# Layer 0's mixers: list scheduling of noted instructions, second parts of weights by adding DMAs, decayed states as products

## The chip, the cores and the metric

The kernel is one program on one core of a Trainium2 chip. A core has five engines with a queue each, worked through in order: TensorE (PE), VectorE (DVE), ScalarE (ACT), GpSimd (POOL) and SyncE (SP, which here only issues DMAs). They meet through semaphores. The metric is the device time of one execution in microseconds, the median of several runs. All times by stage come from one profiled execution.

## The reference, cut to what matters

```python
# layer 0 (even)
z = rmsnorm(h, mix_norm) @ mix_w_in                       # (512, 1024) @ (1024, 3328)
y_a = rwkv7_bidir(z[..., :RWKV_COLS], ...)                # 8 heads x 64, both directions
y_b = hyena_bidir(z[..., RWKV_COLS:], ...)                # 512 channels, long filters by FFT
h = h + concatenate([y_a, y_b], -1) @ mix_w_out
# the scan in rwkv7_bidir, one step
sa = einsum('dbhvk,dbhk->dbhv', S, kk_t)
S = S * w_t[..., None, :] - sa[..., :, None] * (kk_t * a_t)[..., None, :] + v_t[..., :, None] * k_t[..., None, :]
y_t = einsum('dbhvk,dbhk->dbhv', S, r_t)
# the rest, after the mixers of layer 0
h = h + conv_ffn(h, ...); h = h + per_layer_embedding(h, ...)
# layer 1: neighbourhood attention, conv_ffn, per_layer_embedding in the same manner
```

512 tokens, width 1024, everything in float32. What the change touches is `y_a` and `y_b`, the input projection before them, and some work of later parts that runs beside them.

## The kernel before, in words

**Products in two parts.** A large product is made of float32r matmuls of 128x128 by 128x512. Weights and activations are split in a rounded first part (`xh`, `whi`) and a second part, the rest (`xl`, `wlo`); `mm3` sums three matmuls: first by first, first by second, second by first. In the mixers a weight comes in pieces of 128x512 (256 KB), called items. `stream` loads an item to a slab, ACT casts it to the first part (line 570), and GpSimd subtracts that from the loaded item to get the second (`parts`, a subtraction of line 356). The tables of the transform have both parts in HBM: two loads, a cast on ACT (597) and one on GpSimd (598).

**The mixers.** `mixer0` holds 59 slabs of 128x520 in SBUF and eight PSUM banks. The work is: `norm0` (squares on ACT, their sum over 1024 rows on DVE, four one-column matmuls, then rstd); `low_rank` and `columns` (the projection, 26 column groups of 24 large matmuls, two items each); for each of four head pairs m `rwkv_in`, two `rwkv_prep` (one per direction), `inverse_ab` (a block inverse: 15 steps of row substitution on DVE, then small matmuls; it goes through HBM twice), `scan` and `rwkv_out`; for Hyena `hyena_in`, `filters`, `filter_parts`, `forward`, `signals`, `spectrum`, `inverse`, `hyena_out`; and beside them `embedding` (products of the embeddings for both layers, stored for later) and `out_early` (part of the output projection, from the first three head pairs).

**One chunk of a scan.** A scan goes through 512 tokens in eight chunks of 64, both directions and both heads of a pair at once. In a chunk PE multiplies the state tile `uv` by `m1`, DVE copies the result out of PSUM to `r0` (1267), PE multiplies by the inverse `zt`, ACT and DVE write the negated result to the two halves of `uv` (359, 1282), PE multiplies by the keys `x`, and DVE adds the decayed old state `sp` in two operations, one for each half (`uv<-b,sp`). `sp` itself, the state times the chunk's decay `pcs`, is two multiplications on DVE earlier in the chunk. Up to two scans run at once.

**What sets the order.** All functions are generators. `drive` pulls them: `main` is the list of projections, transforms and embeddings in a written order; `chains` are the other parts with a priority each. `Pace` keeps an estimate of when each engine is free and each tile is done. At each point `drive` takes the first chain whose tiles are ready, or, when PE's recent work is thin, the next step of `main`. `in_order` then fixes that order on each engine.

**The end.** After the mixers `outproj0` loads h back (1539), loads the late rows of the output weight (`wraw<-in_mix_w_out_b`, 378), splits them and multiplies. From there on the program runs feed-forward, embedding, attention and again feed-forward.

Lines: 350 is every `mm`, 353 every `stt`, 356 every `tt`, 359 every `act`, 364 the cast of `split`.

Of the kernel before, what the change touches and what calls it, by code (L numbers as in the profile page):

```python
# [19 lines left out]
P = 128  # L20
# [184 lines left out]
class Pace:  # L205


    HOP, OWN = 0.2, 0.13

    def __init__(self, nc):  # L210
        self.nc = nc
        self.free, self.done, self.used = {}, {}, {}
        self.dma = 0.0
        self.columns = {}
        self.recent = deque()
        self.pending = {}
        self.n = len(nc.cur_bb.bb.instructions)

    @staticmethod
    def name(t):  # L220
        return t if isinstance(t, str) else getattr(t, "tensor", t).name

    @staticmethod
    def area(x):

        size = math.prod(x.tensor.shape[1:])
        p, f = divmod(x.offset, size)
        p1, f1 = p, f
        for i, (step, n) in enumerate(x.ap):
            if i == 0 and step == size:  # L230
                p1 += n - 1
            elif step < 0:
                f += step * (n - 1)
            else:
                f1 += step * (n - 1)
        return x.tensor.name, (p, p1, f, f1)

    def now(self, engine=None):
        self.update()
        return self.free.get((engine or self.nc.tensor).engine, 0.0)  # L240

    def ready(self, tiles):

        self.update()
        return max((math.inf if self.pending.get(n) else max(self.done.get(n, {}).values(), default=0.0)
                    for n in map(self.name, tiles)), default=0.0)

    def after(self, marks, area, e, own):

        t = 0.0  # L250
        name, (p, p1, f, f1) = area
        for (k, (q, q1, g, g1)), v in marks.get(name, {}).items():
            if p <= q1 and q <= p1 and f <= g1 and g <= f1:
                if k != e:
                    t = max(t, v + self.HOP)
                elif own:
                    t = max(t, v + self.OWN)
        return t
# [4 lines left out]
    def cold(self, t):  # L263
        return self.columns.get(int(t / self.TICK) - 1, 0) < self.COLUMNS

    def density(self, t):

        while self.recent and self.recent[0][0] < t - self.TICK:
            self.recent.popleft()
        return sum(c for _, c in self.recent)  # L270

    def cost(self, ins, op, n):
        nc, e = self.nc, ins.engine
        if e == nc.tensor.engine:
            passes = 1 if ins.ins[0].dtype == F32R else 2 if ins.is_transpose else 4
            t = max(n * passes / 2400, 0.214 if n < 8 else 0.0)
            return (t + 0.053) / 2 if ins.tile_size[1] == 64 else t
        if e == nc.gpsimd.engine:
            return 0.1 + n * (0.19 if op == ALU.pow else 0.0022)
        if e == nc.scalar.engine:  # L280
            return 0.08 + n * 0.0009
        return 0.07 + n * 0.00106

    def update(self):
        new = self.nc.cur_bb.bb.instructions[self.n:]
        self.n += len(new)
        for ins in new:
            if not ins.outs:
                continue
            src = [self.area(x.bass_ap) for x in ins.ins if hasattr(x, "bass_ap")]  # L290
            dst = [self.area(x.bass_ap) for x in ins.outs if hasattr(x, "bass_ap")]
            e = None if ins.opcode == "DMACopy" else ins.engine
            t = max([0.0] + [self.after(self.done, x, e, True) for x in src]
                    + [self.after(at, x, e, False) for x in dst for at in (self.done, self.used)])
            n = math.prod(c for _, c in ins.outs[0].ap[1:])
            if e is None:
                t = max(t, self.free.get(ins.engine, 0.0))
                self.free[ins.engine] = t + 0.45
                self.dma = max(self.dma, t) + n * ins.outs[0].ap[0][1] * 4 / 340e3
                end = self.dma + 2.1  # L300
            else:
                t = max(t, self.free.get(e, 0.0))
                c = self.cost(ins, getattr(ins, "op", None), n)
                if e == self.nc.tensor.engine:
                    tick = int(t / self.TICK)
                    rows = src[0][1][1] - src[0][1][0] + 1
                    self.columns[tick] = self.columns.get(tick, 0) + c * 2400 * rows / P
                    self.recent.append((t, c * 2400 * rows / P))
                    if self.cold(t):
                        c *= 2  # L310
                end = self.free[e] = t + c
            for x, at in [(x, self.used) for x in src] + [(x, self.done) for x in dst]:
                at.setdefault(x[0], {})[e, x[1]] = end


class Kern:
# [32 lines left out]
    def mm(self, out, lhsT, rhs, start=True, stop=True):  # L349
        return self.nc.tensor.matmul(out, lhsT, rhs, start=start, stop=stop)  # L350
# [152 lines left out]
    def mixer0(self):  # L503
# [17 lines left out]
        with ExitStack() as st:  # L521
            start = len(nc.cur_bb.bb.instructions)
            self.pace = Pace(nc)
# [12 lines left out]
            self.sl = self.pool(st, "sl", bufs=self.SLABS, side="right")  # L536
            self.pb = self.pool(st, "pb", bufs=8, space=PSUM)
            self.both_mixers()
            self.in_order(start)

    SLABS = 59
    PREPS = 4
# [31 lines left out]
    def stream(self, items):  # L574


        self.loads, self.split_ = deque(), deque()
        todo = iter(items)

        def load():  # L580
            srcs = next(todo, None)
            if srcs is not None:
                t = [self.slab() for _ in srcs]
                for x, y in zip(t, srcs):
                    self.nc.sync.dma_start(out=x, in_=y)
                self.loads.append(t)

        for _ in range(self.LOADS):
            load()
        yield  # L590
        while True:
            t = self.loads.popleft()
            if len(t) == 1:
                r = self.parts(t[0])
            else:
                r = [self.slab(F32R) for _ in t]
                self.nc.scalar.copy(r[0], t[0])
                self.nc.gpsimd.tensor_copy(out=r[1], in_=t[1])
            self.split_.append(r)
            load()  # L600
            yield

    LOADS, AHEAD = 3, 3

    def feed(self, now):
        while self.loads and len(self.split_) < self.AHEAD and self.pace.ready(self.loads[0]) <= now + self.SLACK:
            next(self.ws)

    def item(self):
        if not self.split_:  # L610
            next(self.ws)
        return self.split_.popleft()

    def weights(self, name, g):
# [1225 lines left out]
```

## Time and profile before

| what | us |
|---|---|
| median of three runs (1628.54 to 1631.26) | 1630.37 |
| profiled execution, its own time | 1629.27 |
| its span, first to last instruction | 1627.5 |
| first load of the next stage issued (the mixers' last cast starts beside it) | 507.86 |
| first matmul of the next stage | 515.2 |
| PE busy, first 515.2 us / behind | 439.73 / 1095.64 |
| DVE busy, first 515.2 us / behind | 389.50 / 659.38 |
| ACT busy, first 515.2 us / behind | 203.31 / 476.56 |
| POOL busy, first 515.2 us / behind | 245.68 / 94.88 |
| mean granted clock of PE, first 515.2 us / behind | 0.93 / 0.99 |

Busy time is time in which at least one instruction of the engine runs; matmuls overlap, so the sum of their durations is more than PE's busy time, and a busy PE need not be at its peak. In a group's line stand the source line, engine, operation, output and inputs, count, then busy time, mean duration in ns, and the idle time of the engine just ahead of these instructions with what ended it. The granted clock is the share of its full speed that PE was given. Issuing a DMA isn't counted as busy.

### The profile page before, as it was taken

How to read it: one execution, taken by the hardware profiler on the slowest of the kernel's cores; microseconds unless marked ns; L12 is line 12 of the kernel's file. 1: busy time of each engine (PE TensorE's matmuls, PEld its weight loads, DVE VectorE, ACT ScalarE, POOL GpSimd, SP SyncE). 2: the span in 40 equal slices, each digit the busy share in tenths (PEclk: the TensorE clock that was granted, in tenths of full speed). 3: DMA queues.
4: the chain of work that ended last, by engine and by line, in shares of the span. 5: the costliest groups of instructions: out<-in, count | busy, mean ns of one | idle time of the engine just before them, and what ended most of it. 6: DMA issues, size and time to landing. Idle time of an engine off the chain costs nothing.

```text
span 1627.5 us, 24082 instructions
## 1 busy us (share of the span) xinstructions
PE 1535.4 (94%) x9296; PEld 1217.3 (75%) x9296; DVE 1048.9 (64%) x1740; ACT 679.9 (42%) x1082; POOL 340.6 (21%) x286
## 2 busy tenths in 40 slices
PE   6998888988987999999999999999999999999998
PEld 4676665766766888888888878768778888888886
DVE  6579867877774766725774674564675665366654
ACT  6464214333513544423443463664554443244332
POOL 3576525534640300000001223011030000000020
PEclk9999899898998999999999999999999999999999
DMA  6455638365665322232234232323212323222421
GB/s 203 135 137 140 189 89 250 111 197 177 204 220 192 104 97 98 93 102 92 90 103 156 83 126 96 117 79 115 74 58 98 104 91 103 91 83 99 162 97 65
DMA packets 116308, 200.13 MB, mean 123 GB/s; under 512 B 27729, under 2 KB 57297, under 8 KB 116194
## 3 DMA queue, kind: packets, MB, share of 16 engines
q1 hardware_dynamic: 116194, 198.59, 38.0%
q8 instruction: 73, 1.20, 0.3%
q14 instruction: 41, 0.34, 0.1%
HBM read 166.04 MB, written 30.93 MB: 121 GB/s over the span
## 4 chain that ended last, share of the span: by engine, by line
PE 66%; ACT 1%; DVE 1%; DMA 0%; POOL 0%; issue 0%; SPq 0%; DVEq 0%; POOLq 0%; ACTq 0%
PE g L350 62%; PE s L350 1%; PE m L350 1%; PE m L1785 1%; ACT oh L364 0%; DVE ol L356 0%; DMA wraw<-in_mix_w_out_b 0%; PE m L1736 0%; POOL nacc L356 0%; DVE u L356 0%; ACT xh L359 0%; ACT nsq L359 0%; DVE w L353 0%; DVE h L356 0%; SPq L1539 0%
## 5 line engine op out<-in xcount | busy, mean ns | idle before, releaser
L356 DVE TENSOR_TENSOR wlo<-wraw,whi 128x1024 fp32r<-128x1024 f32 x186 | 235.2, 1267 | 322.8 <-ACT whi L364 322.1
L364 ACT CAST whi<-wraw 128x1024 fp32r<-128x1024 f32 x186 | 193.6, 1041 | 420.5 <-PE g L350 406.5
L350 PE MATMUL g<-xh,whi 128*128 128x512 f32 x872 | 341.7, 392 | 11.1 <-ACT whi L364 11.1
L350 PE MATMUL g<-xh,wlo 128*128 128x512 f32 x872 | 340.2, 390 | 0.0
L350 PE MATMUL g<-xl,whi 128*128 128x512 f32 x872 | 340.0, 390 | 0.0
L356 POOL TENSOR_TENSOR w<-w 128x512 fp32r<-128x512 f32 (+2 forms) x142 | 183.4, 1313 | 173.9 <-ACT w L570 115.7
L350 PEld LDWEIGHTS g<-xh,whi 128*128 128x128 f32 x872 | 164.2, 188 | 46.5 <-ACT whi L364 11.3
L350 PEld LDWEIGHTS g<-xh,wlo 128*128 128x128 f32 x872 | 164.1, 188 | 35.3 <-DVE wlo L356 0.8
L350 PEld LDWEIGHTS g<-xl,whi 128*128 128x128 f32 x872 | 164.2, 188 | 33.6
L350 PE MATMUL b<-xh,w 128*128 128x512 f32 x464 | 176.6, 437 | 8.9 <-ACT xh L359 8.9
L356 POOL TENSOR_TENSOR nacc<-nsq 128x512 f32<-128x512 f32 x5 | 9.2, 1833 | 776.2 <-PE g L350 639.6
L350 PE MATMUL b<-w 64*64 64x64 f32 (+6 forms) x1884 | 130.7, 269 | 18.3 <-DVE w L353 8.1
L350 PE MATMUL g<-hh,whi 128*128 128x512 f32 x352 | 137.2, 390 | 0.0
L350 PE MATMUL g<-hl,whi 128*128 128x512 f32 x352 | 137.0, 389 | 0.0
L350 PE MATMUL g<-hh,wlo 128*128 128x512 f32 x352 | 137.0, 389 | 0.0
L353 DVE SCALAR_TENSOR_TENSOR c<-u,prm,c 128x511 f32<-128x511 f32 x176 | 126.2, 745 | 6.5 <-ACT c L359 5.9
L350 PEld LDWEIGHTS b<-w 64*64 64x64 f32 (+4 forms) x1884 | 94.3, 142 | 44.9 <-POOL w L356 11.3
L350 PEld LDWEIGHTS b<-xh,w 128*128 128x128 f32 x464 | 94.2, 203 | 38.6 <-ACT xh L359 9.6
L359 ACT ACTIVATE c<-u,prm 128x512 f32<-128x512 f32 x88 | 70.3, 816 | 70.7 <-DVE u L356 70.7
L350 PE MATMUL b<-xl,w 128*128 128x512 f32 x232 | 97.9, 422 | 0.9 <-DVE xl L353 0.8
L356 DVE TENSOR_TENSOR w<-w 128x512 f32<-128x512 f32 (+16 forms) x127 | 89.9, 717 | 4.2 <-DMA w<-hw_d 1.4
L356 DVE TENSOR_TENSOR u<-g,rstd 128x512 f32<-128x512 f32 x104 | 71.3, 685 | 16.4 <-PE g L350 15.6
(177 smaller groups left out, 2338.9 us busy)
## 6 DMA issues: line engine op xcount, KB each, us to landing
wraw<-in_up SPq DMA_DIRECT2D x88, 512.0 KB, 3.4
wraw<-in_down SPq DMA_DIRECT2D x44, 512.0 KB, 3.5
w<-in_mix_w_in SPq DMA_DIRECT2D x52, 256.0 KB, 3.8
wraw<-in_na_w_qkv SPq DMA_DIRECT2D x24, 512.0 KB, 3.5
x<-ch_d SPq DMA_DIRECT2D x16, 640.0 KB, 5.9
ch_d<-w SPq DMA_DIRECT2D x64, 128.0 KB, 2.7
wraw<-in_gate SPq DMA_DIRECT2D x16, 512.0 KB, 3.4
tab<-in_rpb SPq DMA_DIRECT2D x8, 768.0 KB, 4.3
```

The costliest lines, as they stand in the source:

```text
L350: return self.nc.tensor.matmul(out, lhsT, rhs, start=start, stop=stop)
L353: return self.nc.vector.scalar_tensor_tensor(out=out, in0=in0, scalar=scalar, in1=in1, op0=op0, op1=op1)
L356: return (eng or self.nc.vector).tensor_tensor(out=out, in0=in0, in1=in1, op=op)
L359: return self.nc.scalar.activation(out=out, in_=in_, func=func, **kw)
L364: self.nc.scalar.copy(h, src)
L1785: nc.tensor.transpose(pst[:, i], sc[:, i // 2, (i % 2) * P:(i % 2 + 1) * P], ident)
```

## The change

Four things change, all within `mixer0`.

1. **Order.** `Pace`, `drive` and the generators go. The functions now call recorders: `Plan.note` notes each instruction as a step (several short matmuls in a row make one), with a price, its tiles, and the earlier steps that it depends on. `Plan.schedule` then places all steps by list scheduling: on each engine it takes, among the steps that could start within 0.15 us of the earliest, the one of highest rank. A rank is the longest way to the end of the noted work, plus 1000 times a number for the group (`ORDER`: scans 100, inverses 90, preparations 80, filters 75, ... embeddings 10). A step whose tiles find no free slab has to wait; spans of slab use are reserved per group, so that no group gets stuck half way. `gates` hold a group back until another has got to a point. The calls are made in that order, and `in_order` fixes it as before.
2. **Second parts.** An item is loaded to one of three `wr` tiles. ACT writes its negated rounding, `copy(-1 x item)`, to the second part, GpSimd issues a DMA that adds the item, from HBM a second time, onto that tile, and ACT casts the first part. 70 items do so; 60 of them use 12 tiles `wp` (six pairs), the others slabs. There are 44 slabs instead of 59.
3. **Decayed states.** In a scan, ACT makes diagonal matrices `dg` from the identity and `pcs`; four matmuls add `dg` times the old state to the PSUM bank in which the keys' product is summed later. The new state is then copied out of PSUM, one half by ACT, the other by DVE. `r0` is copied by ACT instead of DVE.
4. **Small ones.** `norm0` sums its squares by 32 one-column matmuls instead of seven additions on DVE and four matmuls; the `+1` of a preparation (line 960) goes from DVE to ACT.

```diff
-class Pace:
+class Plan:
...
+    HOP, OWN, AHEAD = 0.2, 0.1, 0.15
...
+    def ranks(self):
...
+        for s in reversed(self.steps):
+            tail = 2.1 + s.bytes / 340e3 if s.bytes else 0.0
+            s.rank = s.cost + tail + max((t.rank + (0 if t.engine == s.engine else self.HOP) for t in s.then),
+                                         default=0.0)
...
+            for e in engines:
+                c = [(start(s), s) for s in ready[e]]
+                c = [x for x in c if x[0] < math.inf]
+                if not c:
+                    continue
+                m = max(free[e], min(x[0] for x in c)) + self.AHEAD
+                t, s = max((x for x in c if x[0] <= m), key=lambda x: x[1].rank)
+                if best is None or t < best[0]:
+                    best = t, s
...
-    SLABS = 59
+    SLABS, PARTS = 44, 12
+
+    ORDER = dict(start=200, low=190, filters=75, scan=100, inverse=90, prep=80, z=77, out=60, hyena=50,
+                 fparts=40, kf=39, signals=45, ab=58, back=69, early=30, emb=10)
...
+    def item(self, held=False):
+        t = []
+        srcs = self.sources.popleft()
+        for y in srcs:
+            t.append(self.wr.tile([P, S], F32, name="wr"))
+            self.nc.sync.dma_start(out=t[-1], in_=y)
+        if len(t) == 1:
+            r = [self.slab(F32R) if held else self.wp.tile([P, S], F32R, name="wp") for _ in range(2)]
+            self.act(r[1], t[0], AF.Copy, scale=-1.0)
+            self.nc.gpsimd.dma_start(out=r[1], in_=srcs[0], accum_op=ALU.add)
+            self.nc.scalar.copy(r[0], t[0])
+            return r
...
     def norm0(self, xin):
...
+            for t in range(4):
+                self.mm(ps[:, t:t + 1], sq[:, t * P:(t + 1) * P], self.cst("one"), k == t == 0, k == KT - 1 and t == 3,
+                        group=False)
-            if acc is None:
-                acc = sq
-            else:
-                self.tt(acc, acc, sq, ALU.add)
...
     def rwkv_prep(self, m, d, zz):
...
-        nc.vector.tensor_scalar(out=w_, in0=w_, scalar1=1.0, scalar2=None, op0=ALU.add)
+        self.act(w_, w_, bias=1.0)
...
     def scan(self, m):
...
+                dg = dgs[c] = rb.tile([P, 2, P], F32, name="dg", bufs=3)
+                for d in range(2):
+                    self.act(dg[:, d], self.cst("ident"), AF.Copy, scale=self.pcs[:, m, d, c:c + 1])
...
+                        self.mm(ch[rows, d, 2], dg[rows, d, rows], uv[rows, d, par, w], False, group=False)
-            nc.vector.tensor_copy(out=r0, in_=ch[:, :, 0])
+            nc.scalar.copy(r0, ch[:, :, 0])
...
-                sp = rb.tile([P, 2, 64], F32, name="sp", bufs=4)
-                for par, rows in both:
-                    self.tt(sp[rows], uv[rows, :, par, w],
-                            self.pcs[rows, m, :, c].unsqueeze(2).to_broadcast([64, 2, 64]), ALU.mult)
...
-                for par, rows in both:
-                    self.tt(nx[rows, :, par, wn], ch[rows, :, 2], sp[rows], ALU.add)
+                nc.scalar.copy(nx[0:64, :, 0, wn], ch[0:64, :, 2])
+                nc.vector.tensor_copy(out=nx[64:128, :, 1, wn], in_=ch[64:128, :, 2])
```

Three places show how instructions move. The first is GpSimd's queue where the first weights come in, before:

```order
L890 MEMSET w 128x2
L356 ISA
L356 TENSOR_TENSOR w<-w 128x512 x3
L356 TENSOR_TENSOR rr<-rv,epsc 128x4
L356 TENSOR_TENSOR w<-w 128x512 x4
```

and now (`wp` is a second part, `rr` the norm's reciprocal root):

```order
L562 MEMSET w 128x2 x7
L562 DMA wp<-in_mix_w_in 128x512 x3
L562 ISA
L562 TENSOR_TENSOR rr<-rv,epsc 128x4
L562 TENSOR_SCALAR epsc<-prm 128x1
L562 DMA wp<-in_mix_w_in 128x512 x8
```

The subtractions of 128x512 are gone, and in their places stand DMAs that add.

The second is PE's queue at its start, before (`xh`, `xl` are the parts of the normed x, `con` holds the column of ones):

```order
L350 MATMUL b<-xh_215,w 128x512
L350 MATMUL b<-xl_216,w 128x512
L350 MATMUL b<-xh_215,w 128x512
L350 MATMUL b<-xh_236,w 128x512
L350 MATMUL b<-xl_237,w 128x512
```

and now, with the numbers of the buffers:

```order
L562 MATMUL b_207<-xh0_178,wp_209 128x512
L562 MATMUL b_207<-xl0_179,wp_209 128x512
L562 MATMUL b_177<-con_58,w_180 128x1 x4
L562 MATMUL b_177<-con_58,w_183 128x1 x4
...
L562 MATMUL b_177<-con_58,w_201 128x1 x4
L562 MATMUL b_207<-xh0_178,wp_210 128x512
L562 MATMUL b_207<-xh1_181,wp_209 128x512
```

All sums of squares come after two large matmuls now; before, the large matmuls of the first 27 went on and the sums stood behind them.

The third is DVE's queue in one chunk of the first scan, before:

```order
L356 TENSOR_TENSOR uv_2013<-b_2099,sp_2110 64x2x64 x2
L356 TENSOR_TENSOR w_1991<-b_1993,rstd0_145 128x512
L1267 COPY r0_2186<-b_2181 128x128
L356 TENSOR_TENSOR sp_2192<-uv_2013,pcs_144 64x128 x2
L1282 TENSOR_SCALAR uv_2013<-b_2181 64x2x64
```

and now:

```order
L562 COPY uv_330<-b_336 64x2x64
L562 TENSOR_TENSOR w_865<-b_864,w_861 128x512
L562 TENSOR_TENSOR w_844<-b_843,w_840 128x512
L562 TENSOR_TENSOR w_856<-b_855,w_854 128x512
L562 TENSOR_TENSOR w_858<-b_857,w_854 128x512
L562 TENSOR_TENSOR w_849<-b_848,w_847 128x512
L562 TENSOR_SCALAR uv_330<-b_339 64x2x64
```

Of six operations of a chunk on DVE two are left, a copy and a negation, and work of the filters stands between them.

More of the change, by code (lines that the diff above doesn't have):

```diff
@@ L266, in density @@
[L266 to L282, printed above, removed]
@@ L316, with write @@
+    def write(self, order):
+        for s in order:
+            e = getattr(self.nc, s.engine)
+            for method, args, kw in s.calls:
+                getattr(e, method)(*args, **kw)
 class Kern:
@@ L572, in parts @@
         return h, l
[L574 to L612, printed above, removed]
+    def item(self, held=False):
[10 more added lines that the diff above has]
+            return r
+        r = [self.slab(F32R) if held else self.wp.tile([P, S], F32R, name="wp") for _ in range(2)]
+        self.nc.scalar.copy(r[0], t[0])
+        if len(t) == 1:
+            self.tt(r[1], t[0], r[0].bitcast(F32), ALU.subtract, self.nc.gpsimd)
+        else:
+            self.nc.gpsimd.tensor_copy(out=r[1], in_=t[1])
+        return r
     def weights(self, name, g):
```

737 lines of the change are left out of this document (398 added, 339 removed).

## The prediction

> **What bounds the kernel now.** I read the slices of the span first, then busy time by stage, then the chain that ended last.
>
> ```profile
> PE   6998888988987999999999999999999999999998
> DVE  6579867877774766725774674564675665366654
> PEclk9999899898998999999999999999999999999999
> ```
>
> A slice is 1627.5/40 = 40.7 us. After the thirteenth PE is full and its clock unbroken; before it PE has holes and the clock dips. The first 515 us are layer 0's mixers, all that the change touches. The chain dates their end and gives PE's pace in the stage behind:
>
> ```profile
> 507.86 6.22 DMA wraw<-in_mix_w_out_b
> ...
> 515.20 1.22 PE g L350 x2
> ...
> 562.61 354.21 PE g L350 x1560
> ```
>
> 354.21/1560 = 0.227 us for each matmul of 512 columns. From 515.2 on the program is unchanged and PE-bound, so whatever the mixers gain or lose goes into the time one for one. Busy time by stretch (the columns are PE, weight loads, DVE, ACT, POOL, then granted clock, DMA share, GB/s):
>
> ```profile
> 0.00:508.00 508.00, 439.73 (x4160) 325.82 (x4160) 388.37 (x724) 201.80 (x387) 245.68 (x230) 0.94 0.56 171
> 20.00:504.00 484.00, 429.41 (x4138) 319.89 (x4137) 374.11 (x699) 187.58 (x364) 241.50 (x219) 0.93 0.55 167
> 100.00:200.00 100.00, 85.24 (x850) 63.95 (x841) 90.23 (x173) 41.53 (x74) 62.32 (x61) 0.91 0.58 156
> 270.00:380.00 110.00, 94.46 (x1059) 71.93 (x1057) 88.67 (x184) 34.85 (x73) 48.59 (x41) 0.88 0.61 181
> 504.00:515.20 11.20, 0.09 (x1) 0.00 (x1) 5.06 (x9) 3.41 (x5) 0.00 (x0) 0.73 0.80 277
> 0.00:20.00 20.00, 10.23 (x23) 5.94 (x24) 10.33 (x20) 12.32 (x20) 4.17 (x11) 1.00 0.85 265
> ```
>
> Between 20 and 504 us PE idles 484 - 429.4 = 54.6 us, and a clock of 0.93 costs about 0.07 x 429.4 = 30.1 us more: 84.7 us that a better filled PE could have back. In the two stretches where DVE is busiest, 90% and 81%, PE loses 14.8 + 0.09 x 85.2 = 22.4 us and 15.5 + 0.12 x 94.5 = 26.9 us, **49.3** together. The other 274 us lose **35.4**. So the mixers have two limits in turn: PE's own work, and, where preparations and block inverses crowd, DVE.
>
> **The change part by part.**
>
> DVE first. These are its groups in the mixers (count, busy us, mean ns, idle before):
>
> ```profile
> L356 DVE TENSOR_TENSOR w<-w 128x512 f32<-128x512 f32 x51 | 49.2, 981 | 2.5 <-DMA w<-hw_d 1.4 <-ACT w L1300 0.4
> L353 DVE SCALAR_TENSOR_TENSOR w<-w,prm 128x512 f32<-128x512 f32 x38 | 39.8, 1057 | 2.7 <-POOL w L356 2.5
> L356 DVE TENSOR_TENSOR w<-b,w 128x512 f32<-128x512 f32 x40 | 27.3, 685 | 9.6 <-PE b L350 8.8
> L353 DVE SCALAR_TENSOR_TENSOR w<-w,prm,b 128x512 f32<-128x512 f32 x12 | 8.9, 742 | 2.4 <-PE b L932 2.3
> L356 DVE TENSOR_TENSOR sp<-uv,pcs 64x128 f32<-64x128 f32 x56 | 21.2, 378 | 1.3
> L356 DVE TENSOR_TENSOR uv<-b,sp 64x128 f32<-64x128 f32 x56 | 16.0, 286 | 12.4 <-PE b L350 11.3
> L1282 DVE TENSOR_SCALAR uv<-b 64x128 f32<-64x128 f32 x32 | 9.4, 294 | 13.1 <-ACT uv L359 12.2
> L1267 DVE COPY r<-b 128x128 f32<-128x128 f32 x32 | 9.2, 286 | 13.3 <-PE b L350 13.3
> L960 DVE TENSOR_SCALAR w<-w 128x512 f32<-128x512 f32 x8 | 4.6, 580 | 2.8 <-ACT w L359 2.8
> ```
>
> Gone are sp 21.2, the uv additions 16.0, r 9.2, L960 4.6 and seven of the 51 additions (the first norm's sums), 7 x 0.981 = 6.9: 57.9 us. New are 28 copies of half a state, priced like L1282, 8.2 us. Net -49.7.
>
> Then the contention. The same operation takes 981 ns with both inputs in SBUF and 685 with one in PSUM, 1057 against 742 in the fused form: 44 x 0.296 + 38 x 0.315 = 25.0 us of stretching. The timelines of DVE and of GpSimd (start, length) show with what, and GpSimd's group of it follows:
>
> ```profile
> 161.04 3.37 DVE L353 SCALAR_TENSOR_TENSOR w<-w,prm 128x511 f32<-128x511 f32 x2
> ...
> 162.15 1.72 POOL L356 TENSOR_TENSOR w<-w 128x512 fp32r<-128x512 f32 x1
> ...
> L356 POOL TENSOR_TENSOR w<-w 128x512 fp32r<-128x512 f32 x86 | 123.9, 1453 | 146.4 <-ACT w L570 115.7 <-issue 11.7 <-DVE w L356 10.6
> ```
>
> Two fused operations take 1.7 us each while GpSimd subtracts a weight's second part. 70 of these 86 subtractions go, 70 x 1.453 = 101.7 us or 41% of GpSimd's 245.7, so I take 41% of the stretching, 10 us. DVE falls from 388 to 388.4 - 49.7 - 10 = 329 us, 15% less, and in the crowded stretches from 90% to about 76% and from 81% to 68%. PE idles there for DVE's results, though some of that is the chain itself. Between nothing and all of the 49.3 us I take two thirds: **33 us** gained.
>
> The scans and the order. What PE waited for over the mixers (total, times, longest):
>
> ```profile
> PE b L350 <- DVE uv L356: 13.7, 14, 3.3
> PE b L350 <- DVE uv L1282: 5.7, 5, 3.1
> PE b L350 <- DVE r L1267: 4.6, 5, 1.8
> ```
>
> 24.0 us of idling stand behind a scan's evacuations. A chunk's last step was two additions in a row on DVE, 2 x 286 ns; now ACT and DVE copy one half each, so 0.27 us of a chunk's chain goes, 28 x 0.27 = 7.6 us if bare. One scan runs at a time, with matmuls of other parts between its steps, so a chunk can be filled from all open work. I take two fifths of the 35.4 us, between none and all: **14 us** gained.
>
> PE gets 112 matmuls of 64x64 for the decay and 28 more sums of one column. Two groups of PE, and a dense run from its timeline:
>
> ```profile
> L350 PE MATMUL b<-r,w 64*64 64x64 f32 x256 | 15.9, 249 | 5.0 <-DVE r L1267 4.6
> L350 PE MATMUL b<-con,w 128*128 128x1 f32 x40 | 4.8, 242 | 0.2 <-POOL w L890 0.2
> 229.90 1.10 PE L350 MATMUL b<-w 64*64 64x64 f32 x32
> ```
>
> In a scan such a matmul costs 15.9/256 = 62 ns, dense 1.10/32 = 34. By the scan's row 112 x 0.062 = 6.9, and 28 x 4.8/40 = 3.4: **10 us** lost, 7 at the least.
>
> The start. PE's queue now has all 32 one-column sums behind the first two matmuls, so it waits for the last square of x, which ended here:
>
> ```profile
> 18.07 0.61 ACT L359 ACTIVATE w<-w 128x512 f32<-128x512 f32 x1
> ```
>
> PE did 23 matmuls before 20 us; some 20 of them move behind that point, 20 x 0.227 = **4.5 us** lost. Nothing hides it, since no later work has its inputs yet. It could be zero if the sums' earlier end pays it back.
>
> ACT takes over work; its nearest groups:
>
> ```profile
> L570 ACT CAST w<-w 128x512 fp32r<-128x512 f32 x86 | 51.3, 616 | 20.4 <-DMA w<-in_mix_w_in 9.9 <-DVE w L356 5.5 <-DMA w<-in_mix_w_out_a 2.8
> L359 ACT ACTIVATE uv<-b 64x128 f32<-64x128 f32 x32 | 8.6, 270 | 126.9 <-PE b L350 103.7 <-DVE sp L356 23.2
> L1300 ACT COPY w<-b 128x256 f32<-128x256 f32 x16 | 5.2, 376 | 11.5 <-PE b L350 11.5
> ```
>
> 70 negated copies at 0.616 are 43.1 us; 56 diagonals and 32 r0 copies of 128x128, estimated at 0.30 between 0.270 and 0.376, 26.4; 28 half states at 0.27, 7.6; eight +1 at 0.616, 4.9. ACT goes from 201.8 to 284 us of 508, 56%: room, so nothing on the path. But a scan's copy can now queue behind a cast of 0.616 us; that cost is why I don't take more of the 35.4.
>
> The adding DMAs. Each of the 70 second parts is now load, negated copy, and a DMA from GpSimd's queue that adds the weight again from HBM. No such DMA is in this trace; its nearest rows are the plain loads (KB, us from issue to landing) and a plain issue on SP:
>
> ```profile
> w<-in_mix_w_in SPq DMA_DIRECT2D x52, 256.0 KB, 3.8
> x<-ch_d SPq DMA_DIRECT2D x16, 640.0 KB, 5.9
> 491.72 0.38 SPq L1440 DMA_DIRECT2D w<-x_d  x1
> ```
>
> For landing I take 3.8 us, with 5.9 as the nearest longer row; for GpSimd's time an issue between 0.38 and the 1.453 us that it replaces, so GpSimd ends between 171 us and its old 246. 60 of the 70 pairs share twelve buffers, six pairs. PE eats a pair in 12 x 0.227 = 2.7 us, so between a pair's release and its next need lie 6 x 2.7 = 16.3 us. Take off 0.6 for the copy and 2.7 for the use: a DMA has **13 us** before PE notices, and I cost it at nothing. Traffic grows by 70 x 256 KB = 18.4 MB. At today's 171/0.56 = 305 GB/s that is 60 us of DMA time, 120 if a read of the target counts too, on top of 0.56 x 508 = 284: a share of 72% to 85% of some 475 us. It binds in spots only.
>
> Here one rule speaks against the change.
>
> ```profile
> L1089 DVE TENSOR_SCALAR w<-b,prm 128x256 f32<-128x256 f32 x3 | 1.6, 541 | 1.1 <-PE b L350 1.1
> L1096 DVE TENSOR_SCALAR w<-w 128x256 f32<-128x256 f32 x3 | 0.9, 294 | 0.1
> ```
>
> DVE's single-source operation within SBUF runs at almost twice the pace of the one from PSUM. The Trainium skill, "SBUF — State Buffer", section "SBUF: two separate sides", says that while such a faster operation runs GpSimd can't write the descriptors of DMAs that it issues, and "A bandwidth-pool intuition that's wrong" has one going from about 620 to 3100 ns. By that each adding DMA that meets one would land 2.5 us later, and the sum would stand, since 13 us are there. No run here shows it yet.
>
> The tail, 504 to 515.2 us, stays: gates, splits, and the first load of the next stage behind its buffers. I take 0, between 6 us less (the load no longer waits for the last DVE split) and 5 more (the last table's load stands on SP behind stores of the embedding).
>
> **Sum.** 33 + 14 - 10 - 4.5 = 32.5 us. The profiled execution took 1629.27 us (span 1627.5 and 1.8 around it), so **1597 us**; the median of the three runs is 1630.37, 1.1 above it, well within what I can resolve.
>
> **The rivals.** *All lost time comes back.* The 84.7 us between 20 and 504 us nearly vanish. For it: DVE, ACT and GpSimd would all stay under 70%. Against: an order fixed beforehand, on engines that work strictly in order, meets DMAs whose landing it can't know. 84.7 x 0.9 - 10 - 4.5 = 62 us: 1567.
>
> *The gain is given back in new waits.* PE waits for ACT's copies behind casts as it did for DVE's additions, and the new order keeps as much idling as the old: 47 us don't come, 14.5 are paid, half of it hidden in the remaining idle time. 1629 + 7 = 1636 at worst, 1622 where a third of the gain survives; I put it at 1629.
>
> *The adding DMAs land late; this one ends slower.* The place is a run of matmuls on streamed weights, where PE waits for a second part. The price: past 13 us each further microsecond costs 60/6 = 10 us, as six pairs share it. At 13 + 3.25 = 16.3 us the gain is gone; at 18 us the time is 1597 + 50 = 1647. For it: the DMA share is high, and two DMAs and a copy stand in a row where one DMA stood. Against: even 640 KB lands in 5.9 us.
>
> By the skill's rule above the landing would have to be stretched five times over to get there; that adds little to this rival's chance.
>
> **How the numbers follow.** The forecast gets 0.57, with 1580 to 1614 as its own spread; all back 0.17; given back 0.13; late DMAs 0.13. A measurement here can tell 0.2%, 3 us, from no change. Forecast and all-back are faster, and of the given-back case 0.06 faster, 0.05 the same, 0.02 slower: faster 0.80, same 0.05, slower 0.15. The range leaves out about 0.1 on each side: down to 1560, with half of all-back, and up to 1638, with given-back and the milder late DMAs.
>
> **What would show it.** In the profile after, the next stage's first matmul at 515.2 - 32 = 483 us; DVE near 329 us in the mixers; the fused operations near 742 ns where they took 1057; ACT near 284; PE's waits for uv and r under 24 us; adding DMAs landing under 6 us. I am wrong if DVE falls as worked out and PE idles as before (then DVE wasn't the limit), if PE waits for wp behind DMAs, or if the clock stays at 0.93 although PE idles less.

## The result and the profile after

The changed kernel takes 1637.4 us (median of 19 runs) where the kernel before, run on the same chips beside it, takes 1626.8 (19 runs): a ratio of 1.0072, 95% interval 1.0053 to 1.0091. It is 0.7% slower. The prediction had 1597 us. Medians here and below are of all runs, ratios and intervals of the undisturbed ones; two runs lie far outside, 3812 us among the six of the kernel without adding DMAs (the median of its other five is 1600.5) and 5216 us among the ten of the one with alternating subtractions (1618.8).

The profiled execution of the changed kernel spans 1635.6 us. Its page, to be held against the one of before: first slices of the span, then the DMA queues (packets, MB, share of 16 engines).

```profile
PE   8978979988985999999999999999999999999998
DVE  2563646866372677634675575564675666266654
PEclk9987989999998999999999999999999999999999
DMA  8886576798596322232334232423213222323421
...
q1 hardware_dynamic: 116194, 198.59, 37.8%
q0 software_dynamic: 10080, 18.35, 6.7%
```

DVE's digits in the mixers have fallen, as meant; PE's have as many holes as before. The new queue q0, the 70 adding DMAs, took 6.7% of 1635.6, or 109.6 us on all 16 engines, for 18.35 MB.

The end of the mixers, from PE's timeline (start, duration, what ended the idling before it):

```profile
523.11 0.80 PE L599 MATMUL g<-xh,whi 128*128 128x512 f32 x1 [14.18 <-ACT whi L613]
```

Before it was 515.20. These 7.9 us are nearly the whole difference of the two profiled executions (1635.6 - 1627.5 = 8.1); behind this point nothing changed. The mixers as one stretch, of before, then of after (columns as in the prediction: PE, weight loads, DVE, ACT, POOL, clock, DMA share, GB/s):

```profile
0.00:515.20 515.20, 439.73 (x4160) 325.83 (x4161) 389.50 (x726) 203.31 (x388) 245.68 (x230) 0.93 0.57 174
```

```profile
0.00:523.10 523.10, 450.76 (x4440) 330.65 (x4440) 294.04 (x595) 280.32 (x582) 201.10 (x230) 0.94 0.77 206
```

This is the ledger. PE's busy time grew by 11.0 us; its idle time went from 515.2 - 439.7 = 75.5 to 523.1 - 450.8 = 72.3 us, only 3 less, though DVE does 95 us less. What PE waited for says how. The largest waits of after (total, times, longest; L562 is the line where all recorded steps are written, so the rows are told apart by their tiles):

```profile
PE b L562 <- ACT w L562: 16.8, 10, 8.6
PE g L599 <- ACT whi L613: 14.2, 1, 14.2
PE b L562 <- DVE w L562: 9.2, 7, 5.2
PE b L562 <- ACT wp L562: 6.8, 1, 6.8
PE b L562 <- issue: 6.7, 4, 3.5
PE b L562 <- ACT uv L562: 6.5, 3, 3.0
PE b L562 <- DMA wp<-in_proj: 3.2, 2, 1.9
```

Summed over all rows, PE waited 44.4 us for DVE before and 9.5 after, but 23.1 for ACT before and 44.3 after, and 3.2 and 8.7 for DMAs. ACT has 280 of 523 us of work, so its load isn't the limit. It waits itself; here is the group of the 60 negated copies of streamed weights (busy, mean ns, then the idle time ahead of them and what ended it):

```profile
L562 ACT ACTIVATE wp<-wr 128x512 fp32r<-128x512 f32 x60 | 37.0, 626 | 42.3 <-DMA wr<-in_mix_w_in 26.7 <-PE b L562 9.3 <-DMA wr<-in_proj 6.4
```

33 us of ACT's idling ahead of these copies (26.7 + 6.4) ended with the landing of a plain weight load. Landings of after (KB, median us from issue to landing):

```profile
wr<-in_mix_w_in SPq DMA_DIRECT2D x52, 256.0 KB, 4.8
wp<-in_mix_w_in POOLq DMA_DIRECT2D x52, 256.0 KB, 5.6
ch_d<-w SPq DMA_DIRECT2D x64, 128.0 KB, 3.5
...
h_d<-w SPq DMA_DIRECT2D x8, 256.0 KB, 7.3
```

The adding DMA lands in 5.6 us, inside the "under 6" of the prediction. But the plain load had 3.8 before and has 4.8, and the stores that carry data between stages are later too. That suggested two theories: **traffic** (the adding DMAs make every transfer late) and **the order** (the list order with its slots holds PE up). A third, that PE waits for the second parts themselves, is the prediction's own rival.

### The profile page after: what moved, and what is told of

Same layout as the page of the kernel before. It is cut to its first block, busy times and chain, and to the rows that moved or that the text cites. A ratio compares the mean times of both kernels' runs of the same rounds, so it can differ in the third digit from the quotient of the medians.

```text
span 1635.6 us, 24744 instructions
## 1 busy us (share of the span) xinstructions
PE 1546.6 (95%) x9576; PEld 1222.3 (75%) x9576; DVE 953.6 (58%) x1609; ACT 756.8 (46%) x1276; POOL 295.9 (18%) x286
## 3 DMA queue, kind: packets, MB, share of 16 engines
q0 software_dynamic: 10080, 18.35, 6.7%
## 4 chain that ended last, share of the span: by engine, by line
PE 81%; DMA 7%; DVE 4%; ACT 2%; SPq 2%; issue 1%; POOL 1%; DVEq 0%; ACTq 0%; POOLq 0%
PE g L599 61%; PE b L562 16%; DVE w L562 3%; SPq L562 2%; PE s L599 1%; PE m L599 1%; DMA wr<-in_mix_w_in 1%; PE m L1842 1%; ACT w L562 1%; DMA wr<-in_proj 1%; DMA x<-ch_d 1%; DMA wr<-in_dft_i 1%; DMA h_d<-w 1%; DMA w<-nd 1%; POOL w L562 1%
## 5 line engine op out<-in xcount | busy, mean ns | idle before, releaser
L599 PE MATMUL g<-xh,whi 128*128 128x512 f32 x872 | 341.8, 392 | 14.2 <-ACT whi L613 14.2
L562 PE MATMUL b<-xh,wp 128*128 128x512 f32 x416 | 148.4, 424 | 7.6 <-ACT wp L562 6.8
L562 PEld LDWEIGHTS b<-xh,wp 128*128 128x128 f32 x416 | 79.1, 196 | 30.8 <-issue 6.8
L562 PE MATMUL b<-w 64*64 64x128 f32 (+5 forms) x1692 | 86.8, 254 | 14.2 <-DVE w L562 6.5
L562 POOL TENSOR_TENSOR w<-w 128x256 f32<-128x256 f32 (+2 forms) x72 | 84.3, 1221 | 65.1 <-ACT w L562 36.1
L562 PE MATMUL b<-xl,wp 128*128 128x512 f32 x208 | 88.7, 426 | 0.0
L562 PEld LDWEIGHTS b<-w 64*64 64x64 f32 (+4 forms) x1692 | 61.5, 136 | 33.0 <-issue 18.3
L599 PE MATMUL g<-whi,xl 128*128 128x512 f32 x192 | 76.9, 401 | 0.0
```

The source lines that it names most:

```text
L562: getattr(e, method)(*args, **kw)
```

## The experiments

All ran beside the kernel before on the same chip; ratios are to it, with 95% intervals. Its median there was 1624.3 to 1625.8 us.

### Parts alone, and parts undone

Adding DMAs in the kernel before, no other line changed:

```diff
-                r = self.parts(t[0])
+                r = [self.slab(F32R), self.slab(F32R)]
+                self.act(r[1], t[0], AF.Copy, scale=-1.0)
+                self.nc.gpsimd.dma_start(out=r[1], in_=self.srcs.popleft(), accum_op=ALU.add)
+                self.nc.scalar.copy(r[0], t[0])
```

> The kernel before with only the second parts made by adding DMAs; its order, its 59 slabs and its scans as they were. Theory DMA: slower than before by 15 us or more, 1645 or above, with loads landing about 1 us later. Theory order: the old order lives with the DMAs, and DVE, freed of GpSimd's subtractions, makes it faster than before, 1610 to 1625.

1665.3 us, 1.0258 (1.0232 to 1.0284): 40 us slower.

The changed kernel without them, the second parts subtracted by GpSimd as before, and the list order planned anew for that:

```diff
-            self.act(r[1], t[0], AF.Copy, scale=-1.0)
-            self.nc.gpsimd.dma_start(out=r[1], in_=srcs[0], accum_op=ALU.add)
             self.nc.scalar.copy(r[0], t[0])
+            self.tt(r[1], t[0], r[0].bitcast(F32), ALU.subtract, self.nc.gpsimd)
```

> The changed kernel with the second parts made by a subtraction on GpSimd again, so no adding DMAs; order by list scheduling and decayed states as products stay. Theory DMA (the adding DMAs fill the DMA engines, and every other transfer lands later): the DMA share of the mixers falls from 0.77 to about 0.58, loads land in 3.8 us again, and the time falls from 1637 to 1600 or less. Theory order (a fixed order that misjudges landings makes the waits, whatever the traffic): the time stays within 10 us of 1637. GpSimd's port theory (its subtractions are what slowed DVE): DVE goes back up to some 330 us in the mixers and the time to 1610 to 1630.

1656.6 us, 1.0191 (1.017 to 1.0212): slower still, although its loads land in 3.3 us. The same with DVE subtracting:

> As the run before, but the subtraction is done by DVE, 70 x 0.69 = 48 us of it, so that neither the DMA engines nor GpSimd have this work. Theory DMA: 1600 or less, as there; if GpSimd's contention with DVE matters too, below the kernel with GpSimd's subtractions, since 70 x 1.45 us of GpSimd go for 48 us of DVE. Theory order: within 10 us of 1637.

1661.9 us, 1.022 (1.0197 to 1.0242). So putting the adding DMAs into the kernel before costs 40 us, and taking them out of the changed one costs 19 and 24 more. Neither theory alone says both. But these two runs changed the order as well as the DMAs: the scheduler planned again. What PE waited for in the run with GpSimd's subtractions fits that, with one hole of 18 us (total, times, longest):

```profile
PE b L562 <- ACT wp L562: 27.2, 8, 8.3
PE b L562 <- DVE w L562: 23.4, 10, 18.2
```

The decays back on DVE, in the changed kernel (diff: the old lines of `sp`, r0 by DVE):

> The changed kernel with the decayed states made on DVE as before (sp by two multiplications, added by two additions) and r0 copied by DVE; adding DMAs and list scheduling stay. If products for decays help: slower than 1637 by 5 to 10 us. If they cost (PE's 112 matmuls, ACT behind casts): 1630 or less. If a scan's chain is hidden by other work: within 4 us of 1637.

1639.9 us, 1.0101 (1.0077 to 1.0124); the changed kernel had 1.0072. The products are worth some 0.3% there, 2 to 5 us, which two overlapping intervals don't make certain. The products alone, in the kernel before:

```diff
-            nc.vector.tensor_copy(out=r0, in_=ch[:, :, 0])
+            nc.scalar.copy(r0, ch[:, :, 0])
...
-                for par, rows in both:
-                    self.tt(nx[rows, :, par, wn], ch[rows, :, 2], sp[rows], ALU.add)
+                nc.scalar.copy(nx[0:64, :, 0, wn], ch[0:64, :, 2])
+                nc.vector.tensor_copy(out=nx[64:128, :, 1, wn], in_=ch[64:128, :, 2])
```

> The kernel before with one part of the change alone: decayed states as products of diagonal matrices on PE, r0 and half of the next state copied by ACT. Theory 'DVE holds the scans up': PE's idle time before the matmuls that read uv and r (17.8 + 5.0 + 2.7 + 6.1 us before) falls by a half, against 7 to 10 us of added matmuls: 1618 to 1626 us. Rival 'the added products stand on the chain and ACT's copies queue behind its casts': 1629 to 1637.

1645.8 us, 1.0125 (1.0105 to 1.0144). PE's busy time rose by 10.2 us and its waits for DVE fell only from 44.4 to 39.5. And the list order alone, decays and subtractions as before:

> The list order alone: the changed kernel with second parts subtracted on GpSimd and the decays on DVE, both as before. Theory 'the order itself gains, the other parts take it back' (the prediction had 14 us for it): 1610 to 1620 us. Rival 'the list order costs time wherever it stands without the adding DMAs' (1656.6 us with the decays as products, and these were worth 2 to 7 us): 1655 to 1667.

1675.6 us, 1.0309 (1.0286 to 1.0331). Each part alone loses 20 to 50 us, all three together 11. The parts don't add up, and each of these kernels is also another order, since the kernel before, too, chooses its order by estimated times. Four of the six (both with subtractions, the products alone, the order alone) are slower than any theory recorded for them.

### Is the order wrong because its prices are?

The scheduler reckons 2.1 us and 340 GB/s for any DMA. With the landings of the trace in its place:

```diff
-                dma = max(dma, t) + s.bytes / 340e3
-                end = dma + 2.1
+                dma = max(dma, t) + s.bytes / 270e3
+                end = dma + (3.8 if s.engine == "sync" else 4.6)
```

> The changed kernel with one thing altered: the list scheduler prices a DMA as the trace of the changed kernel shows it. It took 2.1 us and 340 GB/s, which is 2.9 us for 256 KB; the profile has 4.8 us for such a load on SP's queue and 5.6 us for an adding DMA, so now 3.8 us (SP) or 4.6 us (GpSimd) and 270 GB/s. Same instructions, another order. Theory 'the list misjudges its DMAs': loads start earlier, PE's waits for weights and for reloaded tiles shrink, the next stage's first matmul comes at 513 us or earlier instead of 523, at most 1627 us. Rival 'the DMAs cost by what they carry, or the waits are on ACT and DVE': 1632 to 1645, no better than the changed kernel.

1658.4 us, 1.0215 (1.019 to 1.0241): 21 us slower than the changed kernel with the same instructions, and slower than both recorded theories. Better prices didn't make a better order here, and two orders of the same instructions differ by 20 us. From here on the order was therefore held fixed: the plan is made as for the changed kernel, and only what is then written differs.

### The adding DMAs in a fixed order

Not issued at all, so that the second parts are the negated copies alone:

```diff
             for method, args, kw in s.calls:
-                getattr(e, method)(*args, **kw)
+                if kw.get("accum_op") is None:
+                    getattr(e, method)(*args, **kw)
```

> The changed kernel, every instruction in the same order, but the 70 adding DMAs are not issued: the second parts are the negated copies alone, so this part of the computation is wrong and left out. It measures the adding DMAs by themselves. Theory 'they cost by landing late and by slowing the other transfers': loads land in about 3.3 us instead of 4.8, DMA share in the mixers falls from 0.77 to about 0.56, first matmul of the next stage at 505 us or earlier, at most 1620 us. Rival 'the order and its dependences hold PE up, the DMAs are hidden': within 5 us of the changed kernel, 1630 to 1642.

1602.3 us, 0.9855 (0.9831 to 0.9878). The adding DMAs cost 1.0072 - 0.9855 = 2.2% or 35 us. The mixers of this run, its end of the mixers, and the same ACT group:

```profile
0.00:484.70 484.70, 443.02 (x4440) 329.70 (x4440) 293.03 (x595) 279.17 (x582) 140.42 (x160) 0.95 0.62 184
```

```profile
484.71 0.80 PE L600 MATMUL g<-xh,whi 128*128 128x512 f32 x1 [10.56 <-ACT whi L614]
```

```profile
L563 ACT ACTIVATE wp<-wr 128x512 fp32r<-128x512 f32 x60 | 36.9, 626 | 33.8 <-PE b L563 15.2 <-DMA wr<-in_mix_w_in 7.4 <-DMA w<-xd 6.0
```

The same instructions on PE, DVE and ACT; PE idles 41.7 us instead of 72.3. Ahead of its negated copies ACT idles 33.8 us where it idled 42.3, and only 7.4 us of that, not 26.7, ended with a load of `in_mix_w_in`. The next stage starts at 484.7 us, where the prediction had 483 for the whole change. Where the 38 us between the two traces arise shows in the matmuls that read `gup`, two records in each of the four `out` parts (min, median, max ns, first and last start). After, then without the adding DMAs:

```profile
L562 PE MATMUL b<-sg,gup x8: 592/592/697, 229.5 to 477.5; 128*128 128x512 f32 x8
```

```profile
L563 PE MATMUL b<-sg,gup x8: 592/592/732, 208.1 to 445.2; 128*128 128x512 f32 x8
```

The lag is 21 us at the first, 32 at the last and 38 at the mixers' end: it builds up over the whole stretch, in no single hole. Nor has it a single carrier. PE's largest waits without the adding DMAs, and both ledgers in us:

```profile
PE b L563 <- ACT w L563: 10.7, 6, 7.7
PE b L563 <- DVE w L563: 7.2, 7, 2.3
PE b L563 <- ACT wp L563: 6.7, 1, 6.7
```

| PE in the mixers | with the adding DMAs | without |
|---|---|---|
| busy | 450.8 | 443.0 |
| waits for ACT | 44.3 | 28.0 |
| waits for DVE | 9.5 | 7.5 |
| waits for DMAs | 8.7 | 4.1 |
| other idling | 9.8 | 2.1 |
| end of the mixers | 523.1 | 484.7 |

The largest part, 16.3 us, comes through ACT, but not through its weight copies themselves (`wp` 6.8 and 6.7); it comes through ACT's other results (`w` 16.8 and 10.7, `uv` 6.5 and none, `whi` 14.2 and 10.6).

How a load gets from there to PE shows in the chain of the changed kernel at its longest such wait, 8.6 us, which ends at 100 us (start, us, what):

```profile
95.75 2.99 DMA wr<-in_mix_w_in
...
98.88 0.47 issue
99.35 0.61 ACT w L562
100.00 0.91 PE b L562 x4
```

PE needs ACT's `w`, which stands in ACT's queue behind work on a weight that had to land first. The same hole is there without the adding DMAs, with 7.7 us.

Now the rival's path against the traffic. All adding DMAs issued, but PE reads a fixed tile as its weights instead of what they wrote (for 66 of the 70 second parts):

```diff
+                if method == "matmul" and args[1].tensor.name in self.seconds:
+                    args = (args[0], self.stand, *args[2:])
                 getattr(e, method)(*args, **kw)
```

> The changed kernel, all 70 adding DMAs issued as before in the same order, but PE doesn't read what they write: each matmul with a second part as its weights (of 66 of the 70) reads a fixed 128x128 tile in its place, so that part of the computation is left out. Only the next copy into the same buffer waits for a landing. It tells PE's wait for a late landing from the traffic. Theory 'traffic: the adding DMAs slow every other transfer': 1630 to 1642 us, like the changed kernel. Theory 'landing: PE and what follows wait for the second part itself': 1600 to 1612, like the run without them.

1636.5 us, 1.0073 (1.0043 to 1.0103): nothing came back. PE's wait for the second parts costs nothing that the interval, some 5 us to either side, would show. The other way round, the step and its waits with 8 KB in place of 256 (the other columns stay negated copies):

```diff
+                if kw.get("accum_op") is not None:
+                    kw = dict(kw, out=kw["out"][:, :16], in_=kw["in_"][:, :16])
```

> The changed kernel in the same order with all 70 adding DMAs and all waits for them, but each adds only the first 16 of 512 columns: 8 KB and not 256 KB (the second parts are wrong beyond). The other half of the test: the step is there, the traffic isn't. Theory 'traffic': 1600 to 1612 us. Theory 'the step itself, issue and a landing of some 2 us or more in the chain, holds PE up': 1620 to 1640.

1607.6 us, 0.9895 (0.9872 to 0.9918): by the ratios 29 of the 35 us are gone with the bytes. And the same bytes without the adding, so that the second part is the weight itself:

```diff
+                if kw.get("accum_op") is not None:
+                    kw = dict(out=kw["out"], in_=kw["in_"])
```

> The changed kernel in the same order, but each adding DMA is a plain DMA of the same 256 KB from the same queue into the same buffer, with the same waits (so the second part is the weight itself, and that part of the computation is wrong). In the changed kernel the adding queue's packets took 6.7% of 1635.6 us on 16 engines, 109.6 us for 18.35 MB or 167 GB/s, against 321 GB/s on SP's queue. Theory 'the adding itself costs, each byte takes an engine about twice as long': the queue's share halves to 3.4% and about half of the 35 us comes back, 1614 to 1625 us. Rival 'any second transfer of these bytes at these moments costs as much, the rate is the same': 1630 to 1642.

1616.5 us, 0.9941 (0.9912 to 0.997). Its queues and landings, then the ones of the 8 KB run:

```profile
q0 software_dynamic: 10080, 18.35, 4.2%
...
wr<-in_mix_w_in SPq DMA_DIRECT2D x52, 256.0 KB, 4.0
wp<-in_mix_w_in POOLq DMA_DIRECT2D x52, 256.0 KB, 4.0
...
h_d<-w SPq DMA_DIRECT2D x8, 256.0 KB, 5.0
```

```profile
q0 software_dynamic: 10080, 0.58, 1.1%
...
wr<-in_mix_w_in SPq DMA_DIRECT2D x52, 256.0 KB, 3.5
```

The three doses, and the cost of each against the run without, worked out from the ratios (each is uncertain by some 5 us):

| second parts | q0's packets on 16 engines | plain load lands | time, cost |
|---|---|---|---|
| none | 0 | 3.4 us | 1602.3 |
| adding, 8 KB | 1.1% x 1608.6 = 17.7 us | 3.5 | 1607.6, +7 |
| plain, 256 KB | 4.2% x 1616.0 = 67.9 us | 4.0 | 1616.5, +14 |
| adding, 256 KB | 6.7% x 1635.6 = 109.6 us | 4.8 | 1637.4, +35 |

In the two runs with 256 KB, between a fifth and a third of the DMA engines' added time comes out as time of the kernel. The 8 KB row can't tell engine time from the step itself, its issue and its waits.

Two other ways in which the step could cost don't fit. Reusing a `wp` buffer before its adding DMA has landed would stop ACT's negated copies, but none of the 42.3 us that ACT idled ahead of them ended so. And GpSimd's queue waits at the issues for ACT's negated copies: 97.6 us in the changed kernel, 107.7 with plain DMAs, 72.2 with 8 KB, which doesn't go with the costs of 35, 14 and 7 us.

### Whole second parts in the same order

The subtraction written where the first part is copied, negated copy and adding DMA left out, order as planned for the changed kernel:

```diff
             self.nc.scalar.copy(r[0], t[0])
+            swap[self.nc.open.n] = [("scalar", "copy", (r[0], t[0]), {}), ("gpsimd", "tensor_tensor", (), dict(
+                out=r[1], in0=t[0], in1=r[0].bitcast(F32), op=ALU.subtract))]
```

> The changed kernel in its own order (planned as with the adding DMAs), but written with other second parts: where the first part is copied, GpSimd then subtracts it from the weight; the negated copies and the adding DMAs are not there. The run without adding DMAs took 1602.3 us. Theory 'the order and the products gain some 25 us, and the adding DMAs take it back': GpSimd gets 70 subtractions of 1.45 us, 101 us more on some 200 of 490, which hides: 1600 to 1615 us. Rival 'GpSimd's subtractions cost as much as the DMAs, in whatever order' (1656.6 us in an order planned for them): 1630 to 1660.

1618.9 us, 0.9967 (0.9952 to 0.9983): faster than both kernels, by 0.3% and 1.1%, and between the two recorded theories. Its mixers, and its longest row of PE's waits:

```profile
0.00:504.00 504.00, 450.31 (x4441) 333.57 (x4441) 322.24 (x595) 242.35 (x512) 238.19 (x230) 0.95 0.60 177
```

```profile
PE b L562 <- DVE w L562: 19.5, 8, 6.3
```

It holds the same instructions as the first run with GpSimd's subtractions, 1656.6 us: 38 us lie in the order alone. Against the run without second parts, DVE's 595 instructions take 322 us where they took 293, and PE's waits for DVE are 21.0 us where they were 7.5: GpSimd's subtractions stretch DVE's work. With DVE subtracting:

> As the kernel with GpSimd's subtractions in the changed kernel's order, but DVE subtracts. DVE gets 70 operations of 0.6 to 1.1 us, 42 to 77 us more on 294. Theory 'adding DMAs are the loss, any engine with room hides a subtraction': 1600 to 1615 us. Rival 'DVE was the limit of the kernel before, and with the subtractions it is so again': 1620 to 1660.

1621.3 us, 0.9975 (0.9958 to 0.9991). Alternately:

> The changed kernel's order with the second parts subtracted alternately by GpSimd (35) and DVE (35). All on GpSimd took 1618.9 us, all on DVE 1621.3, none of either 1602.3 with the negated copies left. Theory 'each engine's load delays what stands behind it, and half the load costs half or less': 1606 to 1615 us. Rival 'what costs is the two steps in a row, copy then subtraction, whoever does them': 1616 to 1623.

1619.0 us, 0.996 (0.9943 to 0.9977). How the subtractions are divided makes no difference that the intervals show, so the 17 us to 1602 don't follow either engine's load. The rival on record for the last run, that the two steps in a row cost whoever does them, gave 1616 to 1623 us and fits the three times; no run tests it further, and the cause of the 17 us stays open.

## Why the prediction was wrong

**The step that failed** is the adding DMAs: "a DMA has 13 us before PE notices, and I cost it at nothing", and "It binds in spots only". They cost 35 us in this order, and the kernel before loses 40 with them. The cover was worked out rightly (5.6 us of landing, and nothing gained when PE doesn't read the result) but for the wrong reader. The price isn't paid on the transfer that was added; it is paid on the others. Loads, stores between stages and reloads share the engines with it, the plain load goes from 3.4 to 4.8 us, a store `h_d<-w` of 256 KB from 2.8 to 7.3 (not every group: the reload `x<-ch_d` lands in 8.0 without them and 7.2 with them). PE gets the delay from several sides, in the ledger above mostly as waits for ACT; which late transfer caused which wait wasn't followed one by one. The sum had the number for it: a share of 72% to 85% (measured 0.77) in a stretch whose stages pass data through DMAs.

This agrees with the Trainium skill, "DMA: Bandwidth & Descriptors", section "Issuing engines are not separate DMA queues": transfers of all issuing engines run on the same 16 DMA engines and interleave.

**The rest of the forecast, term by term.** With the adding DMAs out, order, products and start took 1625.6 to 1602.3, 23 us of the 32.5; but that run has its second parts for free, so its nearness to 1597 confirms nothing; with a subtraction for each 7 us are left.

- *DVE.* Forecast 329 us; it is 294. The groups behind it fell as expected: fused operations, forecast near 742 ns, before 1057:

```profile
L562 DVE SCALAR_TENSOR_TENSOR w<-w,prm 128x512 f32<-128x512 f32 x38 | 28.5, 772 | 9.1 <-ACT w L562 8.9
```

  PE's waits for DVE fell by 35 us, near the 33 of the term. That DVE held PE up was right, and most of what was gained there came back as waits for ACT. The condition "if DVE falls as worked out and PE idles as before (then DVE wasn't the limit)" came true, but its bracket did not: without the adding DMAs the same DVE work leaves PE 34 us less idle than before.
- *The stretching by GpSimd* was put at 10 us; the run with GpSimd's subtractions in the same order shows 29. With that, 16 of the 35 us by which DVE came out lower than forecast stay unexplained.
- *PE's extra work* was put at 10 us, and PE's busy time grew by 11.0, but that nearness is luck: both terms were mis-sized. The trace holds each such matmul twice, so the row of 256 that gave 62 ns holds 128 matmuls, and the row of 40 holds 20. The decay products have 224 records, 13.3 us and not 6.9; the sums of one column grew from 4.8 to 18.0 us, 13.2 and not 3.4. PE's other rows came out 15.5 us lower:

```profile
L562 PE MATMUL b<-uv,dg 64*64 64x64 f32 x224 | 13.3, 240 | 0.0
L562 PE MATMUL b<-con,w 128*128 128x1 f32 x96 | 18.0, 317 | 1.3 <-DMA con<-in_const 1.3
```

- *ACT* at 284 us: 280. PE's waits for it grew by 21 us all the same.
- *GpSimd* was put between 171 and 246 us and has 201. Unlike SP's, its DMA issues are counted as busy: 230 instructions and 201.1 us, against 160 and 140.4 without the adding DMAs.
- *The scans and the order*, +14: waits for uv and r fell from 24.0 us to 6.8, so the waits named there went. The order itself can't be given one number: alone it loses 50 us, and at the same instructions it differs by 21 and by 38.
- *The clock* was 0.93 before, 0.94 after and 0.95 in the run without adding DMAs, from 20 us on, beside 65.7, 64.3 and 33.9 us of PE's idling. So little came back from it.
- *The start* was put at 4.5 us lost and wasn't tried by itself. In the traces PE starts its 29th large matmul of the projection 8.8 us later than before (31.6 against 22.9) and its 66th 2.4 us later (40.0 against 37.6); the term lies between.
- *The tail*, put at 0, lost 3 us: PE's last wait is 14.2 us where it was 11.1.

**The rivals.** "The gain is given back in new waits" named what the trace shows: PE idles as before and waits for ACT in place of DVE; it gave 1622 to 1636 us. But ACT's copies queued behind its casts aren't the whole cause, since without the DMAs the same copies in the same order make PE wait 28.0 us for ACT, not 44.3. "The adding DMAs land late" had the right culprit and the wrong path: it asked for a landing past 13 us, and the loss was there at 5.6.

## What to carry to other kernels

Price an added DMA by the engine time that it takes from all other transfers, not by the slack of its own reader: where the DMA share is near 0.6 already and stages pass data through memory, a fifth to a third of that engine time came back here as kernel time. To find what one part of a change costs under a scheduler, keep the order fixed and leave the part out when it is written; planning again compares two orders. Work taken off the busiest engine helps only until the next thing in line, so look also at what feeds the engine that takes over.

## What was unexpected of the hardware

- An adding DMA takes a DMA engine 1.6 times as long as a plain one with the same bytes, queue and target: 109.6 against 67.9 us, 167 against 270 GB/s, with 10080 packets in each. The prediction had allowed for twice. The Trainium skill, "Collectives: The Full Stack", section "The bandwidth ceiling: the fold count and why AG ≠ RS ≠ AR", says of reducing transfers that an add costs two source reads, and measured a factor of 1.93 there; the direction agrees, the factor here is smaller.
- GpSimd is busy 0.88 us with the issue of an adding DMA, whether it carries 256 KB or 8, and 0.55 us with that of a plain one (medians of 52 each).
- The rule that the prediction weighed, of the Trainium skill, "SBUF — State Buffer", section "SBUF: two separate sides" (a faster DVE operation holds up GpSimd's descriptors), wasn't put to the test. With plain DMAs on both queues the 256 KB landed in 4.0 us from GpSimd's and 4.0 from SP's in the median, but single-source operations within SBUF, the ones that the prediction found faster, fill only some 5 of DVE's 296 us in that run's mixers.
- An 8 KB adding DMA still landed in 3.0 us and took 17.7/70 = 0.25 us of all 16 engines, where one of 256 KB took 109.6/70 = 1.57: a sixth of the time for a thirty-second of the bytes.
